# Reordering the opening of a two-layer diffusion-transformer kernel: one weight load, the modulation units, and the key tiles and first query weights in other buffers

## The chip, the cores and the metric

The kernel runs on one core of one Trainium2 chip. The metric is the device time of one execution in microseconds (us). PE is the matrix engine, DVE the vector engine, ACT the scalar engine, POOL the general engine, SP the engine whose queue issues most DMA transfers. SBUF is the on-chip memory in which tiles lie, PSUM the eight accumulator banks that PE writes.

## The reference

Two layers over 512 latent tokens (stream 0 in the kernel) and 256 context tokens (stream 1), width 1024. Layer 0 is windowed attention with grouped keys, layer 1 retention; each is followed by a SwiGLU. The part that the change touches is the beginning of layer 0:

```python
c_act = jax.nn.silu(c)[:, None, :]
cc_act = jax.nn.silu(c_ctx)[None, None, :]
y_ctx = ctx
for i in range(DEPTH):
    mx = jnp.split(c_act @ ada_w[i] + ada_b[i], 6, axis=-1)
    mc = jnp.split(cc_act @ ada_w[i] + ada_b[i], 6, axis=-1)
    h_x = modulate(rms_norm(x, norm1_g[i]), mx[0], mx[1])
    h_c = modulate(rms_norm(y_ctx, norm1_g[i]), mc[0], mc[1])
...
q_x, k_x, v_x = jnp.split(h_x @ w_qkv, [qd, qd + kvd], axis=-1)
q_x = rope_2d(rms_norm(q_x.reshape(B, S, N_HEADS, HEAD_DIM), q_gain), tables)
k_x = rope_2d(rms_norm(k_x.reshape(B, S, N_KV_HEADS, HEAD_DIM), k_gain), tables)
k_c, v_c = jnp.split(h_c @ w_qkv[:, qd:], 2, axis=-1)
k_c = rms_norm(k_c.reshape(B, L, N_KV_HEADS, HEAD_DIM), k_gain)
```

The other four of the six modulation rows (a gate, then shift, scale and gate for the SwiGLU) are needed only behind the attention. Layer 1 also needs the logarithm of its decay, `log_sigmoid(decay_logit)`, for 8 numbers.

## The kernel before, in words

The time to some 100 us is the opening: all inputs of layer 0 come in, the modulation rows are computed on PE, and keys, values and the first queries are projected. Every float32 product of a projection is made of three matmuls, high weight by high input, low weight by high input, high weight by low input (`mm3`, L143 to L149); a weight tile of 128x1024 is split into a high part by ACT (`whi`, L164 or L382) and a low part by DVE (`wlo`, L165 or L386).

The order on PE, DVE and ACT is written out by hand (L469 to L517, in a manual schedule), and after that for PE alone (L642 to L661), where a scheduler orders the other engines. The pieces, with the short names that the text uses:

- A **quarter** (`ada_quarter`, L337) multiplies four loaded 128x1024 tiles by the two conditioning columns, and gives a quarter of the shift and scale rows of both streams. `columns(1)`, which it returns as `c1`, writes those of the context.
- **U0 to U3** (`ada_unit`, L309): 64 small matmuls each (L315), for the other modulation rows; each unit needs 2 MB of weights. ACT copies the result out (L318). **T0 to T3** are what a unit returns (`finish`): one transpose on PE (L322) and two small additions on DVE (L325).
- **K(s,q)** (`keys`, L445) and **V(s,q)** (`values`, L455): a quarter of the depth of the key and value projections of stream s. In the trace they are L450 and L464; the latent keys go to the PSUM tiles `pj`, the context keys to `pO`, the values to `kvv`.
- **KF0, KF1** (`key_factor`, L540): one matmul (shown as 2 pieces, L542) that sums the squares of a key tile, then on ACT a logarithm, an exponential (both L101) and a square (L198), and on DVE three operations (L199, L200, L545). The key gain (L529, L530) copies key tiles out of PSUM, and `rope_key` (L532) rotates the two latent ones in four DVE operations.
- **q0[0], q0[1], ...** are the pieces of the first query projection. q0[0] is 15 matmuls of 128x512 (L147 to L149). Its weight tile comes raw (`q0_raw`) and is split in four half pieces.
- The **lg chain** (L801 to L819): two ACT operations and 21 small DVE operations on 8 columns. The scheduler puts them where their inputs allow.

Loads are all issued by SP, in program order, and an issue that waits for a buffer holds up all behind it. The quarters, two of the four key/value weights and the units U1 to U3 rotate through 8 buffers with the tag `adan` (128x1024 each); the first two key/value weights lie in `wraw` buffers. U0 comes into the 8 buffers with the tag `k`, which hold keys later. PSUM: quarters, units, transposes and key factors take turns in two banks, `pT`.

The loads stand in this order: quarter 0, three key/value weights, quarter 1, the context, the fourth key/value weight, quarters 2 and 3, the rotation tables, the masks, `q0_raw`, then U0 (8 loads) and U1 to U3 (12). `off_grid` (L228) allocates a narrow filler tile, so that the tiles behind it start at another offset.

Of the kernel before, what the change touches and what calls it, by code (L numbers as in the profile page):

```python
# [8 lines left out]
F32 = mybir.dt.float32  # L9
# [40 lines left out]
def dit_kernel(ctx, tc, xT, cT, crow, small, consts, masks, tabs0, tabs1, jtab, adaQ, adaN, adaT, wst, out):  # L50
# [346 lines left out]
    load_w(st_p, "adan", 8)  # L397
# [70 lines left out]

    with tc.manual_schedule(engines={mybir.EngineType.PE, mybir.EngineType.DVE, mybir.EngineType.Activation}):  # L469
        for n in (SX, SX, SX, SX, 256):  # L470
            busy(n)
        stats0(0)
        c1 = ada_quarter(0, wq[0], lambda: busy(256))
        split_w(st_p)
        busy(SX)
        hidden0(0, 0, 1, between=(split_low,))
        c1()
        split_w(st_p)
        split_low()
        keys(0, 0)  # L480
        split_w(rp)
        split_low()
        squares0(1)
        c1 = ada_quarter(1, wq[1], lambda: values(0, 0, (0, 1)))
        hidden0(0, 2, 3)
        c1()
        values(0, 0, (2, 3))
        rms(1, bank=pT)
        keys(0, 1)
        c1 = ada_quarter(2, wq[2], lambda: values(0, 1, (0, 1)))  # L490
        c1()
        hidden0(1, 0, 1)
        split_w(rp)
        hidden0(1, 2, 3)
        values(0, 1, (2, 3))
        c1 = ada_quarter(3, wq[3], lambda: (keys(1, 0), hidden0(0, 4, 5)))
        c1()
        split_low()
        keys(1, 1)
        hidden0(0, 6, 7)  # L500
        keys(0, 2)
        c1 = ada_unit(UNITS[0], wu[0])
        hidden0(1, 4, 5)
        hidden0(1, 6, 7)
        c1()
        values(1, 0)
        values(1, 1)
        c1 = ada_unit(UNITS[1], wu[1])
        for i, mt in enumerate(mtmp):
            nc.vector.tensor_copy(mask[:, 4 * i * P:4 * i * P + mt.shape[1]], mt)  # L510
        keys(1, 2)
        c1()
        c1 = ada_unit(UNITS[2], wu[2])
        keys(0, 3)
        last_key = keys(1, 3)
        c1()
        c1 = ada_unit(UNITS[3], wu[3])  # L517
# [3 lines left out]
    swap16 = [i + 16 if i < 16 else i - 16 for i in range(32)]  # L521


    kx, kc = {}, {}
    kn = [T(ap, 512, "tt", TTB) for _ in range(3)]
    ksq = [T(ap, 656, "pr", PRB)[:, :512] for _ in range(3)]
    off_grid(ap, 16)
    for a, b, o in zip(kn, ksq, (kvx[0], kvc, kvx[1])):
        nc.scalar.activation(b, o, AF.Square)  # L529
        nc.scalar.activation(a, o, AF.Identity, scale=qk_gain[:, 1:2])  # L530

    def rope_key(t):  # L532

        yy = T(ap, 512, "tt", TTB)
        nc.vector.stream_shuffle(yy, t, swap16)
        nc.vector.tensor_tensor(t, t, rope0[:, 0:512], op=mult)
        nc.vector.tensor_tensor(yy, yy, rope0[:, 512:1024], op=mult)
        nc.vector.tensor_tensor(t, t, yy, op=add)
# [8 lines left out]
    def key_parts(e, src, tag="k", bufs=8):  # L547
        k1, k2 = T(akv, 512, tag, bufs, F32R), T(akv, 512, tag, bufs, F32R)
# [10 lines left out]
    def make_q(j, raw=None):  # L559
# [3 lines left out]
        if raw is None:  # L563
            w = next_w(ap, 0)
            parts_of = lambda k: (w[0][:, k * P:(k + 1) * P], w[1][:, k * P:(k + 1) * P])
        else:

            rows = [[T(ap, 656, "pr", PRB, F32R)[:, :512] for _ in range(2)] for _ in range(2)]
            for i, (hi, lo) in enumerate(rows):
                split(raw[:, i * 512:(i + 1) * 512], hi, lo)  # L570
# [70 lines left out]
    q0 = make_q(0, q0_raw)  # L641
    with tc.manual_schedule(engines={mybir.EngineType.PE}):  # L642
        after(values(0, 2), [last_key])
        c1()
        rope_key(kn[0])
        key_factor(0)
        q0[0]()
        key_factor(1)
# [3 lines left out]
        off_grid(akv, 16)  # L652
        for e in range(2):
            k1, k2 = key_parts(e, kn[1], "kc", 4)
            kc[e], kc[2 + e] = ((k1[:, c], k2[:, c]) for c in HALVES)
        off_grid(akv, 48)
# [145 lines left out]
    after(nc.scalar.activation(t1, dec, AF.Abs), [turn["pre"]])  # L802
# [1161 lines left out]
```

## Time and profile before

| what | value |
|---|---|
| median of 3 runs | 1722.77 us (1722.70 to 1722.93) |
| the profiled execution, its own time | 1725.47 us |
| its span, from the first to the last instruction | 1723.7 us |
| mean granted PE clock in it | 0.998 |
| instructions | 27805 |

A row of the timeline gives the start, the duration from the first start to the last end of the row's instructions, the engine, the line, the operation, the tiles written and read, and the count; in brackets stands how long the engine was idle before it, and what ended that. Matmuls are pipelined, so that a row's duration reaches some tenths into the next row: how long a piece of PE work takes is read from start to start.

### The profile page before, as it was taken

The page shows a single profiled execution, that of the slowest core. Times are in us where ns is not written, and L with a number is a line of the kernel's source. Part 1 is how long each engine was busy: PE and PEld are TensorE (multiplying, and loading weights), DVE is VectorE, ACT ScalarE, POOL GpSimd, SP SyncE. Part 2 cuts the span into 40 slices and gives each one's busy share as a digit, 9 for nine tenths or more (in the row PEclk, how much of TensorE's full clock was granted, in tenths as well). Part 3 has the DMA queues.
Part 4 walks back from the last instruction along what each step waited for, and adds up shares of the span by engine and source line. Part 5 has one row for each costly group of instructions (what it writes and reads, how often), then busy time and mean ns, then how long its engine had stood idle before and what let it go on. Part 6 is the DMA issues. An engine that isn't in the chain of part 4 may idle for free.

```text
span 1723.7 us, 27805 instructions
## 1 busy us (share of the span) xinstructions
PE 1697.5 (98%) x10876; PEld 1514.5 (88%) x10876; DVE 1341.2 (78%) x2418; ACT 867.9 (50%) x1550; POOL 65.7 (4%) x186
## 2 busy tenths in 40 slices
PE   7999999999999999999999999999999999999999
PEld 5788877899999999999988888898898999899988
DVE  6698889788778788787879857757767898877774
ACT  5587779565433334242555534534525564445442
POOL 0000000000000000000000000000000000000000
PEclk9999999999999999999999999999999999999999
DMA  9612221633244534343443624625624323333322
GB/s 351 240 30 58 62 62 56 208 125 125 78 152 122 159 110 147 113 149 118 147 127 84 197 87 122 176 67 132 183 70 121 100 74 117 104 110 111 98 86 86
DMA packets 63378, 209.57 MB, mean 122 GB/s; under 512 B 7312, under 2 KB 8976, under 8 KB 62992
## 3 DMA queue, kind: packets, MB, share of 16 engines
q1 hardware_dynamic: 53168, 171.63, 31.1%
q0 software_dynamic: 9792, 35.66, 8.4%
q8 instruction: 85, 1.39, 0.3%
q10 hardware_dynamic: 288, 0.52, 0.1%
q14 instruction: 45, 0.37, 0.1%
HBM read 201.75 MB, written 2.10 MB: 118 GB/s over the span
## 4 chain that ended last, share of the span: by engine, by line
PE 85%; DVE 6%; DMA 6%; ACT 2%; issue 1%; SPq 0%; DVEq 0%; ACTq 0%
PE Y L897 14%; PE Z L897 7%; PE pj L147 7%; PE pj L149 7%; PE pj L148 7%; PE Z L1296 6%; PE Y L1285 3%; PE X L897 3%; DMA wraw<-in_wst_dram 3%; PE pj L1296 3%; PE pT L736 2%; PE pO L750 2%; PE S L710 2%; PE X L1285 2%; PE X L149 1%; PE X L147 1%
## 5 line engine op out<-in xcount | busy, mean ns | idle before, releaser
L164 ACT CAST whi<-wraw 128x1024 fp32r<-128x1024 f32 x264 | 276.3, 1051 | 337.8 <-PE Z L149 81.3
L165 DVE TENSOR_TENSOR wlo<-wraw,whi 128x1024 fp32r<-128x1024 f32 x264 | 321.5, 1221 | 80.2 <-ACT whi L164 78.5
L897 PE MATMUL Y<-aq,whi 128*128 128x384 f32 x640 | 173.6, 335 | 0.2 <-ACT hn L1053 0.2
L897 PEld LDWEIGHTS Y<-aq,whi 128*128 128x128 f32 x640 | 116.6, 188 | 1.7 <-ACT hn L1053 1.4
L256 DVE SCALAR_TENSOR_TENSOR res<-pj,mod,res 128x512 f32<-128x512 f32 (+1 forms) x112 | 81.1, 728 | 39.6 <-PE pj L149 39.2
L897 PE MATMUL Y<-aq,wlo 128*128 128x384 f32 x320 | 107.0, 334 | 0.0
L273 DVE CUSTOM_DVE_ANT_0 y<-adaw,crow,small_sb 128x1024 bf16<-128x1024 f32 x64 | 81.9, 1280 | 31.7 <-DMA adaw<-in_adaT_dram 31.4
L1296 PE MATMUL Z<-whi,sA 128*128 128x512 f32 x256 | 80.9, 391 | 0.0
L101 ACT ACTIVATE pr<-pr,stat,qs 128x513 f32<-128x513 f32 (+2 forms) x96 | 74.2, 774 | 9.1 <-DVE stat L717 8.8
L147 PE MATMUL pj<-ax,whi 128*128 128x512 f32 x176 | 69.2, 393 | 0.9 <-DVE res L256 0.9
L149 PE MATMUL pj<-ax,whi 128*128 128x512 f32 x176 | 68.7, 390 | 0.0
L148 PE MATMUL pj<-ax,wlo 128*128 128x512 f32 x176 | 68.6, 390 | 0.0
L147 PE MATMUL pj<-act,whi 128*128 128x512 f32 x168 | 65.6, 390 | 0.0
L148 PE MATMUL pj<-act,wlo 128*128 128x512 f32 x168 | 65.6, 390 | 0.0
L149 PE MATMUL pj<-act,whi 128*128 128x512 f32 x168 | 65.5, 391 | 0.0
L897 PEld LDWEIGHTS Y<-aq,wlo 128*128 128x128 f32 x320 | 60.1, 188 | 0.0
L711 DVE CUSTOM_DVE_ANT_0 pr<-S,mask,qs 128x256 f32<-128x256 f32 (+1 forms) x96 | 53.1, 566 | 7.9 <-PE S L710 5.4
L897 PE MATMUL Y<-sA,whi 128*128 128x256 f32 x304 | 58.1, 277 | 0.0
L1296 PEld LDWEIGHTS Z<-whi,sA 128*128 128x128 f32 x256 | 48.0, 188 | 10.4
L897 PE MATMUL Y<-hx,whi 128*128 128x256 f32 x304 | 56.3, 277 | 0.0
L736 PE MATMUL pT<-const_sb,pr 128*128 128x128 f32 x352 | 53.7, 278 | 1.2 <-ACT tt L738 0.9
L1296 PE MATMUL Z<-wlo,sA 128*128 128x512 f32 x128 | 50.4, 394 | 0.5 <-DVE wlo L165 0.5
(580 smaller groups left out, 5051.2 us busy)
## 6 DMA issues: line engine op xcount, KB each, us to landing
wraw<-in_wst_dram SPq DMA_DIRECT2D x224, 512.0 KB, 3.7
adaw<-in_adaT_dram POOLq DMA_DIRECT2D x48, 512.0 KB, 3.8
adan<-in_adaQ_dram SPq DMA_DIRECT2D x16, 512.0 KB, 9.0
wx<-in_wst_dram SPq DMA_DIRECT2D x16, 512.0 KB, 6.4
adan<-in_adaN_dram SPq DMA_DIRECT2D x12, 512.0 KB, 7.7
wx<-in_wst_dram POOLq DMA_DIRECT2D x12, 512.0 KB, 7.4
adaw<-in_adaT_dram SPq DMA_DIRECT2D x8, 512.0 KB, 4.0
wraw<-in_wst_dram POOLq DMA_DIRECT2D x8, 512.0 KB, 5.6
```

Source lines behind the costliest of these rows:

```text
L101: ins = nc.scalar.activation(*args, **kw)
L147: nc.tensor.matmul(o, whi, xhi, start=first, stop=False)
L148: nc.tensor.matmul(o, wlo, xhi, start=False, stop=False)
L149: return nc.tensor.matmul(o, whi, xlo, start=False, stop=last)
L164: after(nc.scalar.copy(hi, t), behind)
L165: return nc.vector.tensor_tensor(lo, t, hi, op=sub)
L256: return nc.vector.scalar_tensor_tensor(res[d], o, mods[l, s][:, part, d:d + 1], res[d], mult, add)
L273: res.append(nc.vector.tensor_tensor_reduce(junk, w, cr[:, s * 1024:(s + 1) * 1024], 1.0, sm_t[:, C_ADAB + l * 48 + j:C_ADAB + l * 48 + j ...
L736: nc.tensor.transpose(tp[:, a * P:(a + 1) * P], self.pr[(0, 2, 1, 3)[a]][:, ki * P:(ki + 1) * P], ident)
L897: nc.tensor.matmul(o, p, r, start=first and k + i == 0, stop=k == 3 and i == 2, skip_group_check=not first)
L1285: ins = nc.tensor.matmul(o[:, e * SC:(e + 1) * SC], p[:, ws], r, start=first and k + e + i == 0, stop=k == 3 and i == 2, skip_group_check= ...
L1296: ins = nc.tensor.matmul(os[t], p, r, start=first and k + i == 0, stop=k == 3 and i == 2, skip_group_check=by_k or not first)
```

## The change

- The **fourth key/value weight** is loaded into a buffer with the tag `kc`, which holds context keys later, and no longer into one of the 8 `adan` buffers. To that end `kc` is two tiles of 1024 columns, where it was four of 512, and the two fillers are allocated at this place.
- The **order of the pieces** in the opening is new: U0 stands behind V(1,0) and V(1,1), T0 and U1 behind K(1,2), T1 behind K(0,3), U2 behind K(1,3), T2 behind V(0,2), and U3, with KF0 inside it, behind that. T3 stands between q0[0] and KF1. The context's first columns (`c1`) come behind a split.
- The **key tiles, their squares, the rotation's temporary and the split first query weights** take `res` tiles, which are free since the inputs have been read, and no longer tiles of the attention's pool, which opens only after the staging pool has closed. So the key gain, the rotation of both latent key tiles and the split of the query weights are in the part that is ordered by hand.
- The **lg chain** is made to run behind the mask copies.

On PE, the place behind K(0,2), which ends with the first row of each list (`h`, `hc` are the normed inputs of the two streams, `k` and `adan` unit weights, `ccol` the conditioning columns, `sq` a unit's rows). Before:

```order
L450 MATMUL pj<-h,whi 128x512 x2
L315 MATMUL pT<-k,ccol 32x128 x32
L322 MATMUL pT<-const_sb,sq 128x128
L464 MATMUL kvv<-whi,hc 128x256
L464 MATMUL kvv<-wlo,hc 128x256
```

Of the change, the end of V(1,1) and what follows:

```order
L466 MATMUL kvv<-wlo,hc 128x256
L466 MATMUL kvv<-whi,hc 128x256
L315 MATMUL pT<-k,ccol 32x128 x32
L452 MATMUL pO<-hc,whi 128x256 x2
L452 MATMUL pO<-hc,wlo 128x256 x2
L452 MATMUL pO<-hc,whi 128x256 x4
L452 MATMUL pO<-hc,wlo 128x256 x2
L452 MATMUL pO<-hc,whi 128x256 x2
L322 MATMUL pT<-const_sb,sq 128x128
L315 MATMUL pT<-adan,ccol 32x128 x32
L452 MATMUL pj<-h,whi 128x512 x2
```

U0 has moved behind both value pieces, and K(1,2) stands between it and its transpose, where before nothing did. (This view counts a unit's 64 matmuls as 32.)

On PE again, the place of KF0. Before:

```order
L464 MATMUL kvv<-wlo,h 128x256
L464 MATMUL kvv<-whi,h 128x256
L322 MATMUL pT<-const_sb,sq 128x128
L542 MATMUL pT<-pr,const_sb 128x512
L147 MATMUL pj<-h,pr 128x512
```

Of the change:

```order
L322 MATMUL pT<-const_sb,sq 128x128
L315 MATMUL pT<-adan,ccol 32x128 x24
L553 MATMUL pT<-res,const_sb 128x512
L315 MATMUL pT<-adan,ccol 32x128 x8
L147 MATMUL pj<-h,res 128x512
```

The transpose before KF0 is now T2, and U3, which stood ahead of V(0,2), surrounds KF0. T3 has gone behind the 15 matmuls of q0[0].

On ACT, the stretch from the key gain to the logarithm of KF1 (`whi<-wraw` is the high part of the second query weights). Before:

```order
L530 ACTIVATE tt<-pj,qk_gain 128x512
L164 CAST pr<-wraw 128x512
L164 CAST whi<-wraw 128x1024
L164 CAST pr<-wraw 128x512
L101 ACTIVATE pr<-pT,small_sb 128x512
L101 ACTIVATE pr<-pr 128x512
L198 ACTIVATE pr<-pr 128x512
L101 ACTIVATE pr<-pT,small_sb 128x512
```

Of the change:

```order
L476 ACTIVATE res<-pj,qk_gain 128x512
L318 COPY sq<-pT 128x128
L101 ACTIVATE pr<-pT,small_sb 128x512
L101 ACTIVATE pr<-pr 128x512
L164 CAST whi<-wraw 128x1024
L198 ACTIVATE res<-pr 128x512
L101 ACTIVATE pr<-pT,small_sb 128x512
```

The two halves of the first query weights are gone from here (they are split earlier), U3's copy stands ahead of KF0's logarithm, and the whole cast of the second query weights stands ahead of KF0's square. On DVE the low part of the second query weights (L165, 128x1024) stands right ahead of the first operation of KF0 (L199), as the rows of the change show:

```order
L165 TENSOR_TENSOR wlo<-wraw,whi 128x1024
L199 SCALAR_TENSOR_TENSOR res<-pT,res 128x512
L325 TENSOR_TENSOR mod_74<-pT,small_sb 128x4
L200 SCALAR_TENSOR_TENSOR pr<-res,pr 128x512
L325 TENSOR_TENSOR mod_75<-pT,small_sb 128x4
L556 TENSOR_TENSOR res<-res,pr 128x512
```

L199 reads KF0's sums in PSUM, so KF0's bank is free only behind it.

The diff (`...` marks what is left out):

```diff
--- before.py
+++ after.py
@@ -394,7 +394,9 @@
     load_w(st_p, "adan", 8)
     wq.append(ada_quarter_load(1))
     res0[1] = load_stream(1)
-    load_w(st_p, "adan", 8)
+    off_grid(akv, 16)
+    load_w(akv, "kc", 2)
+    off_grid(akv, 48)
     wq += [ada_quarter_load(2), ada_quarter_load(3)]
     rope0 = T(akv, 1024, "rope0", 1)
     nc.sync.dma_start(rope0.rearrange("p (a n) -> p a n", a=2), tabs0)
@@ -466,6 +468,21 @@
                     first = first or ins
         return first
 
+    swap16 = [i + 16 if i < 16 else i - 16 for i in range(32)]
+    row = lambda dt=F32: T(rp, 512, "res", 12, dt)
+
+    def key_gain(i, o):
+        nc.scalar.activation(ksq[i], o, AF.Square)
+        nc.scalar.activation(kn[i], o, AF.Identity, scale=qk_gain[:, 1:2])
+
+    def rope_key(t):
+
+        yy = row()
+        nc.vector.stream_shuffle(yy, t, swap16)
+        nc.vector.tensor_tensor(t, t, rope0[:, 0:512], op=mult)
+        nc.vector.tensor_tensor(yy, yy, rope0[:, 512:1024], op=mult)
+        nc.vector.tensor_tensor(t, t, yy, op=add)
+
     with tc.manual_schedule(engines={mybir.EngineType.PE, mybir.EngineType.DVE, mybir.EngineType.Activation}):
         for n in (SX, SX, SX, SX, 256):
             busy(n)
@@ -474,9 +491,9 @@
         split_w(st_p)
         busy(SX)
         hidden0(0, 0, 1, between=(split_low,))
-        c1()
         split_w(st_p)
         split_low()
+        c1()
         keys(0, 0)
         split_w(rp)
         split_low()
@@ -499,43 +516,37 @@
         keys(1, 1)
         hidden0(0, 6, 7)
         keys(0, 2)
-        c1 = ada_unit(UNITS[0], wu[0])
+        values(1, 0)
+        values(1, 1)
         hidden0(1, 4, 5)
         hidden0(1, 6, 7)
+        c1 = ada_unit(UNITS[0], wu[0])
+        keys(1, 2)
         c1()
-        values(1, 0)
-        values(1, 1)
         c1 = ada_unit(UNITS[1], wu[1])
         for i, mt in enumerate(mtmp):
-            nc.vector.tensor_copy(mask[:, 4 * i * P:4 * i * P + mt.shape[1]], mt)
-        keys(1, 2)
+            mask_end = nc.vector.tensor_copy(mask[:, 4 * i * P:4 * i * P + mt.shape[1]], mt)
+        q0_rows = [(row(F32R), row(F32R)) for _ in range(2)]
+        for i, (hi, lo) in enumerate(q0_rows):
+            split(q0_raw[:, i * 512:(i + 1) * 512], hi, lo)
+        keys(0, 3)
         c1()
+        last_key = keys(1, 3)
+        kn, ksq = [row(), row(), row()], [row(), row(), row()]
+        key_gain(0, kvx[0])
+        rope_key(kn[0])
         c1 = ada_unit(UNITS[2], wu[2])
-        keys(0, 3)
-        last_key = keys(1, 3)
+        key_gain(1, kvc)
+        key_gain(2, kvx[1])
+        values(0, 2)
         c1()
         c1 = ada_unit(UNITS[3], wu[3])
     St.close()
     At = ExitStack()
     ap = At.enter_context(tc.tile_pool(name="ap", bufs=1, reuse_waits="tile"))
-    swap16 = [i + 16 if i < 16 else i - 16 for i in range(32)]
-
 
     kx, kc = {}, {}
-    kn = [T(ap, 512, "tt", TTB) for _ in range(3)]
-    ksq = [T(ap, 656, "pr", PRB)[:, :512] for _ in range(3)]
     off_grid(ap, 16)
-    for a, b, o in zip(kn, ksq, (kvx[0], kvc, kvx[1])):
-        nc.scalar.activation(b, o, AF.Square)
-        nc.scalar.activation(a, o, AF.Identity, scale=qk_gain[:, 1:2])
-
-    def rope_key(t):
-
-        yy = T(ap, 512, "tt", TTB)
-        nc.vector.stream_shuffle(yy, t, swap16)
-        nc.vector.tensor_tensor(t, t, rope0[:, 0:512], op=mult)
-        nc.vector.tensor_tensor(yy, yy, rope0[:, 512:1024], op=mult)
-        nc.vector.tensor_tensor(t, t, yy, op=add)
 
@@ -545,7 +556,11 @@
         nc.vector.tensor_tensor(kn[i], kn[i], y, op=mult)
 
     def key_parts(e, src, tag="k", bufs=8):
-        k1, k2 = T(akv, 512, tag, bufs, F32R), T(akv, 512, tag, bufs, F32R)
+        if tag == "kc":
+            both = T(akv, 1024, tag, bufs, F32R)
+            k1, k2 = both[:, 0:512], both[:, 512:1024]
+        else:
+            k1, k2 = T(akv, 512, tag, bufs, F32R), T(akv, 512, tag, bufs, F32R)
         src = src[64 * e:64 * e + 64, :]
         nc.scalar.copy(k1[0:64, :], src)
         nc.scalar.copy(k2[64:128, :], src)
@@ -556,18 +571,14 @@
 
     q, stats = {}, {}
 
-    def make_q(j, raw=None):
-
-
-
-        if raw is None:
+    def make_q(j, rows=None):
+
+
+
+        if rows is None:
             w = next_w(ap, 0)
             parts_of = lambda k: (w[0][:, k * P:(k + 1) * P], w[1][:, k * P:(k + 1) * P])
         else:
-
-            rows = [[T(ap, 656, "pr", PRB, F32R)[:, :512] for _ in range(2)] for _ in range(2)]
-            for i, (hi, lo) in enumerate(rows):
-                split(raw[:, i * 512:(i + 1) * 512], hi, lo)
             parts_of = lambda k: [t[:, k % 4 * P:(k % 4 + 1) * P] for t in rows[k // 4]]
         qs = T(ap, 64, "qs", 4)[:, 0:36].rearrange("p (f n) -> p f n", f=3)
         sqs, o = [], [None, None]
@@ -638,22 +649,18 @@
 
         return [first, second, third, norms]
 
-    q0 = make_q(0, q0_raw)
+    q0 = make_q(0, q0_rows)
     with tc.manual_schedule(engines={mybir.EngineType.PE}):
-        after(values(0, 2), [last_key])
-        c1()
-        rope_key(kn[0])
         key_factor(0)
         q0[0]()
+        c1()
         key_factor(1)
         for e in range(2):
             kx[e] = key_parts(e, kn[0])
         q0[1]()
-        off_grid(akv, 16)
         for e in range(2):
-            k1, k2 = key_parts(e, kn[1], "kc", 4)
+            k1, k2 = key_parts(e, kn[1], "kc", 2)
             kc[e], kc[2 + e] = ((k1[:, c], k2[:, c]) for c in HALVES)
-        off_grid(akv, 48)
         q0[2]()
         values(0, 3)
         q0[3]()
@@ -799,7 +806,7 @@
     t1 = cp.tile([P, 8], F32, name="lg_t1")
     t2 = cp.tile([P, 8], F32, name="lg_t2")
     t3 = cp.tile([P, 8], F32, name="lg_t3")
-    after(nc.scalar.activation(t1, dec, AF.Abs), [turn["pre"]])
+    after(nc.scalar.activation(t1, dec, AF.Abs), [turn["pre"], mask_end])
     lnexp(t1, t1, AF.Exp, scale=-1.0)
     nc.vector.tensor_scalar(t2, t1, 2.0, None, op0=add)
     nc.vector.reciprocal(t2, t2)
```

## The prediction, before the result was known

> **What bounds the kernel now.** First the page, for the engines' shares:
>
> ```profile
> span 1723.7 us, 27805 instructions
> PE 1697.5 (98%) x10876; PEld 1514.5 (88%) x10876; DVE 1341.2 (78%) x2418; ACT 867.9 (50%) x1550; POOL 65.7 (4%) x186
> ```
>
> PE is busy for all but 26 us. What an edit of the opening can bring is a part of those 26 us, or of PE time that is stretched. So I read the chain of waits through the opening next (start, duration, what ran):
>
> ```profile
> 15.30 9.36 DMA res<-in_cT_dram
> ...
> 35.24 0.62 PE pT L345 x16
> 35.88 0.33 SPq L334
> ...
> 50.97 9.98 DMA adan<-in_adaN_dram
> ```
>
> It has three parts. First the context's load sets the pace: it lands at 24.68, and its squares and the rest follow. Then PE works up to quarter 2, and at 35.88 SP issues a load that had waited for quarter 2's first matmuls. All later loads stand behind that issue, and the last of them, U2's weights, lands at 60.95. Two stretches (columns: length, busy time and instructions of PE, weight loads, DVE, ACT, POOL, then granted clock, DMA share, GB/s) show the loads' side:
>
> ```profile
> 35.00:38.00 3.00, 3.00 (x74) 2.63 (x73) 0.00 (x0) 0.37 (x1) 0.00 (x0) 1.00 0.46 137
> 45.00:65.00 20.00, 18.25 (x264) 14.55 (x263) 10.46 (x28) 4.82 (x11) 0.00 (x0) 1.00 1.03 413
> ```
>
> Around the late issue the DMA engines are half empty for 3 us (a share of 0.46, so about 1.6 us of transfer lost); from 45 to 65 they are full at 413 GB/s, while PE idles. The third view is PE's timeline, start to start:
>
> ```profile
> 48.59 1.53 PE L315 MATMUL pT<-k,ccol 128*32 128x128 f32 x48
> ...
> 50.94 0.43 PE L315 MATMUL pT<-k,ccol 128*32 128x128 f32 x8 [0.18 <-DMA k<-in_adaN_dram]
> ...
> 51.89 0.36 PE L464 MATMUL kvv<-whi,hc 128*128 128x256 f32 x1
> ...
> 54.89 1.96 PE L315 MATMUL pT<-adan,ccol 128*32 128x128 f32 x64
> 56.77 0.50 PE L450 MATMUL pO<-hc,whi 128*128 128x256 f32 x2
> ...
> 58.49 1.08 PE L315 MATMUL pT<-adan,ccol 128*32 128x128 f32 x32
> ...
> 61.56 0.74 PE L450 MATMUL pj<-h,whi 128*128 128x512 f32 x2
> ...
> 64.46 0.40 PE L450 MATMUL pO<-hc,whi 128*128 128x256 f32 x2
> ...
> 66.08 1.96 PE L315 MATMUL pT<-adan,ccol 128*32 128x128 f32 x64
> 67.96 0.39 PE L464 MATMUL kvv<-whi,h 128*128 128x256 f32 x1
> ...
> 71.05 1.02 PE L542 MATMUL pT<-pr,const_sb 128*128 128x512 f32 x2
> ...
> 72.91 0.51 PE L148 MATMUL pj<-h,pr 128*128 128x512 f32 x1 [0.23 <-DVE pr L165]
> ...
> 76.25 1.02 PE L542 MATMUL pT<-pr,const_sb 128*128 128x512 f32 x2
> ```
>
> An undisturbed unit takes 1.88 us (54.89 to 56.77, and 66.08 to 67.96). U0 with T0 took 3.30 (48.59 to 51.89) and U2 took 3.07 (58.49 to 61.56): these two wait for weights, T0 also for a copy of U0's rows. The third wait is in q0[0], which stands until DVE has made the query weights' low part (72.91).
>
> **The change, part by part.**
>
> *Ahead of 48.59: nothing.* The first columns and the lg chain move out of the way of stream 0, before 24.68. Whatever is won there waits for the same context load, whose place in SP's queue stays. The fourth weight's load and the loads behind it come a little earlier, but PE's work to 48.59 hangs on the context. I take 0; the bounds are 0 and 0.5 us either way.
>
> *From 48.59 to the end of U3: 2.6 us.* The pieces are the same, in the order V(1,0) V(1,1), U0, K(1,2) T0, U1, K(0,3), T1 K(1,3), U2, V(0,2) T2, U3. By the rows above they take 3.00 + 1.88 + 1.72 + 1.88 + 2.90 + 1.62 + 1.88 + 3.09 + 1.88 = 19.85 us if none waits, against 22.46 (48.59 to 71.05). So U3 would end at 68.44 without KF0, instead of 71.05 with T3: 2.61 us. None has to wait for weights: U0's last piece had landed at 50.9 even with the late issue (its matmuls then start, behind the DMA), and U0 is wanted from 51.6 on; U2's at 60.95, and wanted at 61.6 (48.59 + 3.00 + 1.88 + 1.72 + 1.88 + 2.90 + 1.62). The fourth weight's buffer, which lets the loads run some 1.6 us ahead, is only a margin on that. A transpose's copy is covered by the key piece ahead of it.
>
> *KF0 and q0[0]: 0.9 us.* They took 5.20 us (71.05 to 76.25). KF0 is 0.86 and a matmul 0.23 by the chain's rows:
>
> ```profile
> 76.41 0.86 PE pT L542 x2
> 77.27 0.23 PE pj L147
> ```
>
> That makes 0.86 + 15 x 0.23 = 4.31; the rest was the wait for the split, which is now made before 62. So KF1 could start at 68.44 + 4.31 + 0.2 (T3, one matmul of less width, so somewhat less than 0.23) = 72.95, where it stood at 76.25.
>
> *A new wait at KF1: 1.1 us back.* The two `pT` banks are taken in turn by U3, KF0, T3 and KF1, so KF1 gets KF0's bank, and must wait for L199 of KF0 on DVE. What stands ahead of L199 is priced by these rows:
>
> ```profile
> 68.15 0.27 ACT L318 COPY sq<-pT 128x128 f32<-128x128 f32 x1 [6.13 <-PE pT L315]
> 68.31 0.60 ACT L529 ACTIVATE pr<-pj 128x512 f32<-128x512 f32 x1
> ...
> 71.97 1.10 ACT L164 CAST whi<-wraw 128x1024 fp32r<-128x1024 f32 x1
> ...
> 73.44 0.74 ACT L101 ACTIVATE pr<-pT,small_sb 128x512 f32<-128x512 f32 x1
> 74.22 0.63 ACT L101 ACTIVATE pr<-pr 128x512 f32<-128x512 f32 x1
> ```
>
> ```profile
> 73.37 1.22 DVE L165 TENSOR_TENSOR wlo<-wraw,whi 128x1024 fp32r<-128x1024 f32 x1
> ...
> 77.09 0.68 DVE L199 SCALAR_TENSOR_TENSOR pr<-pT,pr 128x512 f32<-128x512 f32 x1
> ```
>
> U3 now ends behind KF0, at 68.44 + 0.86 = 69.30. Its copy starts 0.19 later (68.15 against 67.96), the logarithm 0.16 behind that (69.65), the exponential 0.78 on (70.43), the cast of the second query weights 0.63 on (71.06); it takes 1.10, their low part 1.22, and L199 0.68: 74.1. PE is there at 72.95 and stands for about 1.1 us. KF1 starts at 74.1 and not 76.25: **a lead of 2.15 us**. Behind it q0[1] and the rest stand in the same order on PE as before, and no engine's work there begins at a time of its own; the lead is kept.
>
> *DVE's load, hidden.* DVE now makes the lg chain, the split's low parts and two rotations between 55 and 69. The prices:
>
> ```profile
> 13.97 1.78 DVE L811 SCALAR_TENSOR_TENSOR lg_t<-lg_t,lg_t 128x8 f32<-128x8 f32 x9
> ```
>
> ```profile
> 55.31 0.69 DVE L510 CAST mask<-hn 128x512 bf16<-128x512 f32 x2
> ...
> 69.53 0.75 DVE L535 STREAM_SHUFFLE tt<-tt 128x512 f32<-128x512 f32 x1
> ...
> 71.43 0.69 DVE L536 TENSOR_TENSOR tt<-tt,rope 128x512 f32<-128x512 f32 x1
> ```
>
> T0's additions end near 55.3, the masks at 56.2, the lg chain (21 operations at 0.20) at 60.5, two low parts of 0.69 at 61.9. The first key tile comes from ACT at 62.7; its rotation (0.75 + 3 x 0.69) ends at 65.5, the second one's shuffle at 66.3. T2 reaches DVE at 66.6. So there are about 0.3 us of slack at T2, and 1.1 more until KF0 wants T2's bank (at 68.0, 24 of U3's 32 steps behind 66.56). At the low part (72.2) the slack is 3 us.
>
> *Addresses.* Tiles of the attention's pool start at other offsets, and the trace of before can't show what these cost. The nearest rows are the score products, which read two kinds of key tiles, at different offsets:
>
> ```profile
> L710 PE MATMUL S<-kc,q x192: 274/282/580, 99.8 to 301.6; 128*128 128x256 f32 x192
> L710 PE MATMUL S<-k,q x128: 274/336/449, 99.5 to 301.8; 128*128 128x256 f32 x64, 128*128 128x384 f32 x64
> ```
>
> Their shortest durations agree to the nanosecond. I take 0, and 0.3 us either way.
>
> *The clock.* PE's granted clock falls to a half in one later place, behind a wait for DVE:
>
> ```profile
> 254.49 0.47 PE L710 MATMUL S<-kc,q 128*128 128x256 f32 x2 [2.53 <-DVE qs L620]
> ```
>
> ```profile
> 253.20:256.60 3.40, 1.34 (x6) 0.89 (x6) 3.37 (x16) 1.71 (x4) 0.00 (x0) 1.00 0.13 49
> 256.60:260.00 3.40, 3.21 (x14) 2.85 (x14) 2.89 (x15) 3.34 (x8) 0.00 (x0) 0.50 0.01 2
> ```
>
> The half clock comes behind 3.4 us in which PE was busy for 1.34. With the work 2.15 us earlier the wait of 2.53 lies from about 249.8 to 252.3. If the grid of such stretches stays where it is, it is in the one from 249.8 to 253.2, which is then just as empty: the slow stretch comes too, only sooner in the work. I take 0. If the wait were cut in two by an edge, the slow stretch would go: at most half of 3.4, 1.7 us.
>
> [...]
>
> **The sum.** 2.61 + 0.89 - 0.2 - 1.15 = 2.15 us. Against the profiled execution that is 1725.47 - 2.15 = 1723.3 us, with a span of 1721.5; that execution lies 2.7 us over the median of the runs shown, so against the median it is 1722.77 - 2.15 = **1720.6 us**. A measurement of this kernel can tell about 0.2% from no change, which is 3.4 us: the forecast lies within it.
>
> **The rivals.**
>
> *B, no wait at KF1.* If ACT's casts run sooner, or DVE gets to L199 before the low part, the lead at KF1 is all of 3.3 us: 1719.5. Against it stand the written orders; for it, that the steps of 0.16, 0.78 and 0.63 come from places with other neighbours. 0.13.
>
> *C, the slow stretch goes* with the forecast's lead: 1720.6 - 1.7 = 1718.9. For it, that its place hangs on a tenth of a microsecond at 249.8; against it, that a wait shifted by less than a stretch is empty somewhere. 0.08.
>
> *D, the change doesn't do what it says.* U0 and U2 wait as before, since the loads land later with PE's wait gone from among them, and only q0[0]'s 0.9 is kept (1721.9), or the lead is lost to a later wait (1722.8). For it, DMA at 1.03 of its share; against it, that the loads keep their order, and margins of 0.7 us with the old times. 0.12.
>
> *E, slower: DVE becomes the bound of the opening.* Place: T2's additions, which free KF0's bank. DVE has 12.5 us of work there in the 13.8 us from 55.2 to 69.0. The first 1.4 us of delay (0.3 + 1.1) are free, the next 2.15 eat the lead; from 3.6 us on each costs its own length. If those operations take 40% longer than their rows (5 us), the result is 1.4 us slower: 1724.2; at 60% (7.5 us) it is 1726.7. Against it, the rows of each kind are known. 0.06.
>
> **How the numbers follow.** The forecast has 0.61: 1720.6, with its own unknown terms 1719.8 to 1721.4. The range, 1718.7 to 1723.0, takes in B, C and D, and leaves out E and the far ends of B and C. Faster by over 0.2% means below 1719.3: C and a third of B, 0.12. Slower by over 0.2% means over 1726.2: half of E, 0.03. The rest, 0.85, lies within.
>
> **What would show it.** In the changed profile: the first row of V(1,0) where U0 stood, within 0.5 us of 48.6; no wait longer than 0.2 us for `k` or `adan` in L315; SP issuing the rotation tables well ahead of 36; U3's first row near 66.6, KF0 near 68.0; q0[0]'s rows unbroken; a wait of about 1 us in front of KF1 that DVE's L199 ends, and KF1 at 74.1. The time would be wrong if that lead of 2.15 us isn't found again at the first scores (99.5 before), if PE waits for `pT` at KF0, or if the half clock near 256 has gone.

## The result, and the profile after

| | before | changed |
|---|---|---|
| median of 22 runs | 1723.86 us (1722.01 to 1726.83) | 1721.36 us (1719.92 to 1723.85) |
| ratio, 95% interval | | 0.9985 (0.9979 to 0.9991) |
| profiled execution: own time, span | 1725.47, 1723.7 | 1722.00, 1720.1 |

The change makes the kernel 2.5 us faster by the medians; the interval of the ratio is 1.6 to 3.6 us. The forecast was 2.15 us. (The median of before is 1.1 us above that of its first three runs, so 1721.36 and the predicted 1720.6 differ by more than the two gains do.) The forecast put the change within the 0.2% that it took for the limit of a measurement; it is 0.15% by the medians, and with 22 runs of each the whole interval of the ratio lies below 1. The two profiled spans differ by 3.6 us, and the sections below show how much of that is the change.

The page and the two stretches of the opening, in the changed kernel:

```profile
span 1720.1 us, 27800 instructions
PE 1695.5 (99%) x10876; PEld 1516.3 (88%) x10876; DVE 1342.2 (78%) x2418; ACT 867.4 (50%) x1550; POOL 65.6 (4%) x186
```

```profile
35.00:38.00 3.00, 3.00 (x72) 2.45 (x72) 0.00 (x0) 0.37 (x1) 0.00 (x0) 1.00 1.02 415
45.00:65.00 20.00, 19.84 (x283) 17.37 (x283) 17.71 (x56) 8.42 (x20) 0.11 (x1) 1.00 0.94 367
```

From 35 to 38 the DMA engines are full (a share of 1.02, where it was 0.46), and from 45 to 65 PE is busy for 19.84 us of 20, where it was 18.25. DVE's 17.71 was 10.46: the lg chain, the split and a rotation have come in. SP issues the rotation tables at 29.86, where it was 36.25. PE's timeline:

```profile
48.73 0.28 PE L466 MATMUL kvv<-whi,hc 128*128 128x256 f32 x1
...
51.65 1.95 PE L315 MATMUL pT<-k,ccol 128*32 128x128 f32 x64
53.53 0.50 PE L452 MATMUL pO<-hc,whi 128*128 128x256 f32 x2
...
55.17 0.33 PE L322 MATMUL pT<-const_sb,sq 128*128 128x128 f32 x1
55.42 1.96 PE L315 MATMUL pT<-adan,ccol 128*32 128x128 f32 x64
...
61.74 1.96 PE L315 MATMUL pT<-adan,ccol 128*32 128x128 f32 x64
63.63 0.39 PE L466 MATMUL kvv<-whi,h 128*128 128x256 f32 x1
...
66.80 1.52 PE L315 MATMUL pT<-adan,ccol 128*32 128x128 f32 x48
68.25 1.12 PE L553 MATMUL pT<-res,const_sb 128*128 128x512 f32 x2
69.30 0.65 PE L315 MATMUL pT<-adan,ccol 128*32 128x128 f32 x16
69.88 0.50 PE L147 MATMUL pj<-h,res 128*128 128x512 f32 x1
...
73.44 0.27 PE L322 MATMUL pT<-const_sb,sq 128*128 128x128 f32 x1
74.44 1.12 PE L553 MATMUL pT<-res,const_sb 128*128 128x512 f32 x2 [0.73 <-DVE res L199]
```

Units stand in single rows of 64 without a bracket: U0 takes 1.88 us (51.65 to 53.53) and U2 1.89. q0[0] runs from 69.88 without a wait, and KF0 doesn't wait for its bank. KF1 waits for DVE's L199, as predicted, but for 0.73 us where 1.15 was forecast, and stands at 74.44. ACT and DVE ahead of it:

```profile
70.07 0.27 ACT L318 COPY sq<-pT 128x128 f32<-128x128 f32 x1 [3.90 <-PE pT L315]
70.23 0.69 ACT L101 ACTIVATE pr<-pT,small_sb 128x512 f32<-128x512 f32 x1
70.96 0.63 ACT L101 ACTIVATE pr<-pr 128x512 f32<-128x512 f32 x1
71.50 1.03 ACT L164 CAST whi<-wraw 128x1024 fp32r<-128x1024 f32 x1
```

```profile
72.56 1.23 DVE L165 TENSOR_TENSOR wlo<-wraw,whi 128x1024 fp32r<-128x1024 f32 x1 [3.49 <-ACT whi L164]
73.70 0.68 DVE L199 SCALAR_TENSOR_TENSOR res<-pT,res 128x512 f32<-128x512 f32 x1
```

This is the forecast chain, link by link: its first link comes 0.6 us later than forecast, its last 0.3. How far the lead gets is seen in the score products, whose row gives the first and the last start (99.5 to 301.8 before):

```profile
L717 PE MATMUL S<-k,q x128: 274/337/449, 97.8 to 300.5; 128*128 128x256 f32 x64, 128*128 128x384 f32 x64
```

The lead is 1.7 us at the first and 1.3 at the last. The missing 0.4 and the rest of the 3.6 us come up below.

### The profile page after: what moved, and what is told of

It is laid out like the page before. It is cut to its first block, busy times and chain, and to the rows that moved or that the text cites. A ratio compares the mean times of both kernels' runs of the same rounds, so it can differ in the third digit from the quotient of the medians.

```text
span 1720.1 us, 27800 instructions
## 1 busy us (share of the span) xinstructions
PE 1695.5 (99%) x10876; PEld 1516.3 (88%) x10876; DVE 1342.2 (78%) x2418; ACT 867.4 (50%) x1550; POOL 65.6 (4%) x186
## 4 chain that ended last, share of the span: by engine, by line
PE 90%; DVE 4%; DMA 2%; ACT 2%; issue 1%; SPq 0%; DVEq 0%; ACTq 0%
PE Y L904 16%; PE Z L904 8%; PE pj L147 7%; PE pj L149 7%; PE pj L148 7%; PE Z L1303 7%; PE X L904 4%; PE Y L1292 4%; PE pj L1303 3%; PE pT L743 2%; PE pO L757 2%; PE S L717 2%; PE X L1292 2%; DMA wraw<-in_wst_dram 1%; PE X L149 1%; PE X L147 1%
## 5 line engine op out<-in xcount | busy, mean ns | idle before, releaser
L165 DVE TENSOR_TENSOR wlo<-wraw,whi 128x1024 fp32r<-128x1024 f32 x264 | 321.5, 1222 | 84.1 <-ACT whi L164 82.8
L743 PEld LDWEIGHTS pT<-const_sb,pr 128*128 128x128 f32 x352 | 40.2, 142 | 12.1 <-issue 4.0
```

The source lines that it names most:

```text
L165: return nc.vector.tensor_tensor(lo, t, hi, op=sub)
L743: nc.tensor.transpose(tp[:, a * P:(a + 1) * P], self.pr[(0, 2, 1, 3)[a]][:, ki * P:(ki + 1) * P], ident)
```

## The experiments

When K(0,2) ends differs between the profiles, from 47.4 to 49.6 us (by 0.3 and 0.9 us between two profiles of one kernel). So absolute places in the expectations below, such as "KF1 at 74.4", are met or missed by this shift too, and the opening is compared by the **stretch from the end of K(0,2) to KF1**: 27.66 us before (48.59 to 76.25) and 25.71 in the changed kernel (48.73 to 74.44). Every ratio below is to runs of the kernel before on the same chip, with its 95% interval; 0.0009 of it is 1.6 us, so that these intervals can't tell one version from the next. The stretch is read from one profile of each version; two profiles of one kernel differ in it by 0.24 and 0.04 us.

| kernel | stretch | ratio |
|---|---|---|
| before; once more | 27.66; 27.42 | 1 |
| changed; once more | 25.71; 25.75 | 0.9985 (0.9979 to 0.9991) |
| e1, fourth weight in adan | 25.72 | 0.9992 (0.9984 to 1.0001) |
| e2, kc buffer alone | 25.63 | 0.9986 (0.9977 to 0.9995) |
| e3, T3 behind q0[1] | 24.69 | 0.9981 (0.9972 to 0.9990) |
| e4, query weights split late | 26.38 | 0.9989 (0.9980 to 0.9998) |
| e5, units at their old places | 24.72 | 0.9986 (0.9977 to 0.9995) |
| e6, masks copied five times | 25.69 | 0.9990 (0.9982 to 0.9999) |
| e7, lg chain early | 25.73 | 0.9980 (0.9971 to 0.9989) |
| e8, res tiles and late lg chain alone | 26.13 | 0.9994 (0.9985 to 1.0002) |
| e9, U2 and U3 earlier | 26.18 | 0.9989 (0.9980 to 0.9998) |

### e1: the buffer undone

```diff
-    off_grid(akv, 16)
-    load_w(akv, "kc", 2)
-    off_grid(akv, 48)
+    load_w(st_p, "adan", 8)
```

(The context key tiles are four of 512 columns again.)

> The changed kernel with one part undone: the fourth key/value weight goes back into an adan buffer, and kc is four tiles of 512 again. Theory (the order of the pieces makes the gain, the buffer is only a margin): no wait over 0.3 us for unit weights in L315, U2 near 61.7, KF1 at 74.4 +- 0.3 as in the changed kernel, first score at 97.8 +- 0.3, time equal to the changed kernel's (ratio to before about 0.9985). Rival (the earlier loads make the gain): U2 waits 0.7 us or more, KF1 at 75.2 or later, and more than half of the gain is gone.

The stretch is 25.72 against 25.71 (all of it 1.3 us earlier, since K(0,2) ended at 47.44 here), and PE's view has no wait for a unit's weights:

```profile
60.45 1.95 PE L315 MATMUL pT<-adan,ccol 128*32 128x128 f32 x64
...
73.16 1.13 PE L551 MATMUL pT<-res,const_sb 128*128 128x512 f32 x2 [0.74 <-DVE res L199]
```

With the new order the earlier loads bring nothing: the theory held in the trace. Its clause on the time is not borne out or refuted; the interval reaches from 1.0001 to below the changed kernel's ratio.

### e2: the buffer alone

The kernel before with the diff of e1 the other way round.

> The kernel before with one part of the change: the fourth key/value weight in a kc buffer. Theory: the waits for U0's and U2's weights vanish (0.21 + 0.18 + 0.19 + 0.58 = 1.16 us in the trace of before), T0's wait of 0.44 for its copy and the wait in q0[0] for the low part stay; KF1 at 75.1 +- 0.3, against 76.25 before, first score at 98.4, about 1.1 us faster. Rival (the DMA engines are the limit and the earlier issue moves nothing): KF1 at 76.2, no gain. Rival (the buffer is the whole gain): KF1 at 74.5.

```profile
51.31 0.33 PE L322 MATMUL pT<-const_sb,sq 128*128 128x128 f32 x1 [0.44 <-ACT sq L318]
...
57.97 1.95 PE L315 MATMUL pT<-adan,ccol 128*32 128x128 f32 x64
...
71.21 0.50 PE L148 MATMUL pj<-h,pr 128*128 128x512 f32 x1 [0.23 <-DVE pr L165]
...
74.54 1.02 PE L544 MATMUL pT<-pr,const_sb 128*128 128x512 f32 x2
```

The weights' waits are gone, T0's wait for its copy and q0[0]'s for the low part stay, as the theory had it; but the gain is 2.0 us and not 1.1. I had added the brackets of PE's rows. By starts, U0 with T0 took 2.48 (3.30 before) and U2 1.88 (3.07): 0.82 + 1.19 = 2.01. A bracket is only the time in which nothing was running. Before, the 32 matmuls ahead of U2's first wait took 1.08 us to their last end, where half an undisturbed unit takes 0.94: two breaks cost U0 with T0 0.82 us where their brackets make 0.39, and two cost U2 1.19 where theirs make 0.77. Matmuls in a run overlap (an undisturbed unit's row lasts 1.96 us, and the next piece starts at 1.88); across a bracket they don't.

So the buffer alone does as much for the stretch as the whole change. With e1, where the order does it without the buffer, this shows that the two remove the same weight waits by two routes.

### e8: the res tiles alone

The kernel before with the res tiles and the late lg chain; loads and PE's order as before.

> Only the res tiles and the later lg chain: fourth weight in adan, kc four tiles, PE in the order of before (T3 ahead of KF0). Theory: all weight waits of before stay, KF0 at 71.05 +- 0.3, q0[0] without its wait, so KF1 at 75.4 +- 0.3, without a bank wait since T3 stands between; about 0.9 us faster than before. Rival (DVE's added work or the chain behind KF0 eats it): KF1 at 76.2, no gain.

```profile
59.12 0.64 PE L315 MATMUL pT<-adan,ccol 128*32 128x128 f32 x16 [0.53 <-DMA adan<-in_adaN_dram]
...
70.38 1.02 PE L551 MATMUL pT<-res,const_sb 128*128 128x512 f32 x2
...
74.69 1.02 PE L551 MATMUL pT<-res,const_sb 128*128 128x512 f32 x2
```

KF0 to KF1 takes 4.31 us, to the hundredth what the prediction worked out, where it took 5.20: the term of 0.89 is right. U2 still waits for its weights. KF0 came at 70.38 and not at 71.05: U0's weights came in time in this execution, and it took 2.48 us with T0 where it took 3.30; U2 took 3.42 where it took 3.07. That makes 0.47 of the remaining 0.64 us (27.66 - 26.13 - 0.89), and the value and key pieces, some hundredths shorter each, make the other 0.17. The loads are those of before, and the second profile of before has one wait for U0's weights where the first has two, so that this part varies without an edit.

### e5: the units at their old places

```diff
         keys(0, 2)
+        c1 = ada_unit(UNITS[0], wu[0])
+        hidden0(1, 4, 5)
+        hidden0(1, 6, 7)
+        c1()
         values(1, 0)
         values(1, 1)
-        hidden0(1, 4, 5)
-        hidden0(1, 6, 7)
-        c1 = ada_unit(UNITS[0], wu[0])
-        keys(1, 2)
-        c1()
         c1 = ada_unit(UNITS[1], wu[1])
...
+        keys(1, 2)
+        c1()
+        c1 = ada_unit(UNITS[2], wu[2])
         keys(0, 3)
-        c1()
         last_key = keys(1, 3)
...
-        c1 = ada_unit(UNITS[2], wu[2])
+        c1()
+        c1 = ada_unit(UNITS[3], wu[3])
         key_gain(1, kvc)
         key_gain(2, kvx[1])
         values(0, 2)
-        c1()
-        c1 = ada_unit(UNITS[3], wu[3])
```

> The changed kernel with the units at their places of before (U0 and T0 ahead of V(1,0), U1 ahead of K(1,2), U2 ahead of K(0,3), U3 ahead of V(0,2)); the kc buffer, the res tiles and T3 behind q0[0] are kept. Theory (KF1's wait for its bank is the bound of this stretch, and DVE's and ACT's chain behind KF0 sets KF1): T0 waits 0.6 to 0.8 us for its copy, but KF0 ends within 0.3 us of where it ends in the changed kernel, and KF1 still stands at 74.5 +- 0.3, with a bank wait of about 0.7; time as the changed kernel's. Rival (each wait removed from PE counts in full): KF1 at 75.1 or later.

Neither theory nor rival: the stretch is 24.72, a microsecond **shorter** than in the changed kernel.

```profile
50.51 0.33 PE L322 MATMUL pT<-const_sb,sq 128*128 128x128 f32 x1 [0.44 <-ACT sq L318]
...
68.42 1.02 PE L553 MATMUL pT<-res,const_sb 128*128 128x512 f32 x2
...
72.83 1.02 PE L553 MATMUL pT<-res,const_sb 128*128 128x512 f32 x2
```

```profile
65.64 0.27 ACT L318 COPY sq<-pT 128x128 f32<-128x128 f32 x1 [3.70 <-PE pT L315]
...
67.91 1.08 ACT L164 CAST whi<-wraw 128x1024 fp32r<-128x1024 f32 x1
69.48 0.69 ACT L101 ACTIVATE pr<-pT,small_sb 128x512 f32<-128x512 f32 x1 [0.49 <-PE pT L553]
```

```profile
71.94 0.68 DVE L199 SCALAR_TENSOR_TENSOR res<-pT,res 128x512 f32<-128x512 f32 x1
```

T0 waits for its copy, as expected, and KF0 comes 20.3 us behind K(0,2)'s end, where it is 19.5 in the changed kernel. But with U3 ahead of V(0,2) ACT copies U3's rows almost 3 us before KF0, and makes the cast of the second query weights while PE is still at the values: at 67.91, ahead of KF0's logarithm. The cast no longer stands between that logarithm and the square, L199 ends at 72.62, and KF1 follows at 72.83 without a wait, with 0.2 us to spare. My theory had kept the changed kernel's order on ACT, which the scheduler doesn't. So the wait at KF1 hangs on the place of U3 around KF0, and **the new order of the units costs the stretch 1.0 us once the buffer is there**. The times can't show this: the ratio is 0.9986, the changed kernel's 0.9985.

### e3: T3 behind q0[1]

```diff
         q0[0]()
-        c1()
         key_factor(1)
         for e in range(2):
             kx[e] = key_parts(e, kn[0])
         q0[1]()
+        c1()
```

> The changed kernel with T3 moved from behind q0[0] to behind q0[1], so that KF1 gets U3's bank, not KF0's. Theory (KF1 waits for L199 only because of the bank): no wait at KF1, KF1 at 73.5 +- 0.2 where it stood at 74.44, first score at 97.0 +- 0.3 (97.81), 0.7 to 0.8 us faster than the changed kernel. Rival (the wait only moves on, to T3 or to the first scores): first score at 97.7, no gain.

```profile
73.02 1.02 PE L553 MATMUL pT<-res,const_sb 128*128 128x512 f32 x2
...
77.02 0.27 PE L322 MATMUL pT<-const_sb,sq 128*128 128x128 f32 x1
```

KF1 waits no more. The stretch is 24.69, 1.02 us shorter, of which 0.27 is T3's own time (73.44 to 74.44 in the changed kernel, less the wait of 0.73), which comes later; at the first score product 0.67 us is left (48.41 from K(0,2)'s end, 49.08 in the changed kernel). U3's place is the same as in the changed kernel, and L199 still ends behind KF1's start (73.29 + 0.68 = 73.97 against 73.02). Only KF1's bank differs: it was the bank.

### e4: the query weights split late

```diff
-        q0_rows = [(row(F32R), row(F32R)) for _ in range(2)]
-        for i, (hi, lo) in enumerate(q0_rows):
-            split(q0_raw[:, i * 512:(i + 1) * 512], hi, lo)
+        [(row(F32R), row(F32R)) for _ in range(2)]
...
+    q0_rows = [[T(ap, 656, "pr", PRB, F32R)[:, :512] for _ in range(2)] for _ in range(2)]
+    for i, (hi, lo) in enumerate(q0_rows):
+        split(q0_raw[:, i * 512:(i + 1) * 512], hi, lo)
```

> The changed kernel with the first query weights split late again, in tiles of the attention's pool; everything else as changed. Theory: ACT makes the two half casts and the whole cast ahead of KF0's logarithm, so q0[0] waits 1.0 to 1.5 us for the low part, and KF0's L199 ends 0.6 to 0.9 us later; KF1 at 75.2 +- 0.3, about 0.8 us slower than the changed kernel. Rival (the early split is worth its whole 0.9 plus the bank wait): KF1 at 75.8 or later. Rival (hidden): KF1 at 74.4.

```profile
71.63 0.50 PE L147 MATMUL pj<-h,pr 128*128 128x512 f32 x1 [0.96 <-ACT pr L164]
72.35 0.50 PE L148 MATMUL pj<-h,pr 128*128 128x512 f32 x1 [0.23 <-DVE pr L165]
...
75.83 1.03 PE L551 MATMUL pT<-res,const_sb 128*128 128x512 f32 x2
```

(The four `res` tiles stay allocated, unused.) The stretch is 26.38, 0.67 us longer: q0[0] waits 0.96 + 0.23, and the bank's wait at KF1 has gone, since PE is late itself. The two waits don't add.

### e6 and e7: DVE's load

```diff
-        for i, mt in enumerate(mtmp):
+        for i, mt in 5 * list(enumerate(mtmp)):
```

> The changed kernel with the two mask copies made five times on DVE, which puts about 2.5 us more of work ahead of the lg chain, the low parts and the rotations (the result is the same). By the working of the prediction DVE has 1.4 us of room there, so KF0 would be 1.1 us late, and KF1 at 75.5. By the trace of the changed kernel the room is larger (2.0 us idle before the second rotation, and 1.1 until KF0 wants the bank): KF0 at 68.2 and KF1 at 74.4, no loss.

The stretch is 25.69. From the first mask copy to the lg chain it is 3.02 us on DVE, where it was 0.60: 2.4 us more of DVE work cost nothing. The prediction's room of 1.4 us was too small, and the trace of the changed kernel shows why:

```profile
59.49 0.68 ACT L476 ACTIVATE res<-pj,qk_gain 128x512 f32<-128x512 f32 x1
```

```profile
66.21 0.01 DVE L481 LOAD_MASK_SELECT res<-res  x1 [2.03 <-ACT res L476]
```

The first key tile's gain is done on ACT at 60.2 (I had 62.7): ACT starts on the tile at 59.00, while PE still works on K(0,3)'s second tile. DVE is through with the first rotation at 64.2 and then waits 2.03 us for the second tile. e7 takes the lg chain out of its new place:

```diff
-    after(nc.scalar.activation(t1, dec, AF.Abs), [turn["pre"], mask_end])
+    after(nc.scalar.activation(t1, dec, AF.Abs), [turn["pre"]])
```

> The changed kernel with the lg chain free to run early again, as before. Theory (hidden at both places): K(0,2) ends at 48.6 +- 0.3 and KF1 stands at 74.4 +- 0.3; no difference in time. Rival (the chain delays stream 0, or its move frees the opening): the rows ahead of 48.7 come 0.4 us later or more.

K(0,2) ends at 48.83 and the stretch is 25.73. That part of the change does nothing here.

### e9: U2 and U3 earlier

```diff
         c1()
+        c1 = ada_unit(UNITS[2], wu[2])
         last_key = keys(1, 3)
...
         rope_key(kn[0])
-        c1 = ada_unit(UNITS[2], wu[2])
+        c1()
+        c1 = ada_unit(UNITS[3], wu[3])
         key_gain(1, kvc)
         key_gain(2, kvx[1])
         values(0, 2)
-        c1()
-        c1 = ada_unit(UNITS[3], wu[3])
```

(T3 stands as in e3. In PE's order KF0 and the first matmul of q0[0] come along: they stand inside U3, and so ahead of V(0,2): KF0 at 66.33, V(0,2) from 68.16.)

> The changed kernel with U2 ahead of K(1,3), T2 and U3 ahead of V(0,2), and T3 behind q0[1]; the kc buffer and the res tiles as changed. Counted from the end of K(0,2) to KF1 (27.66 in the kernel before, 25.71 in the changed one, 24.72 with the old places of the units), theory (with U3 ahead of V(0,2), ACT's chain behind KF0 runs while PE works on the values, and no bank is waited for): 23.4 to 23.9 us, no wait over 0.2 us on PE in between, first score about 1.7 us earlier than in the changed kernel, ratio to before about 0.997 to 0.998. Rival (U2's weights aren't there yet, or KF0 waits for T2's bank): a wait in L315 or at KF0, and 24.5 or more.

The rival came:

```profile
66.33 1.10 PE L553 MATMUL pT<-res,const_sb 128*128 128x512 f32 x2 [1.42 <-DVE mod L325]
```

```profile
63.24 0.75 DVE L481 STREAM_SHUFFLE res<-res 128x512 f32<-128x512 f32 x1
...
65.97 0.23 DVE L325 TENSOR_TENSOR mod<-pT,small_sb 128x4 f32<-128x4 f32 x2
```

KF0 waits 1.42 us for T2's bank, which T2's additions free; they stand on DVE behind the first rotation. That rotation starts at 63.24, where it was 61.40 in the changed kernel, since ACT's order now puts U2's copy (61.85) ahead of the first key tile's square and gain (from 62.01). This is the place that the prediction named for its slower case. There a small operation holds up PE as soon as T2 comes before the rotation's end; in the changed kernel T2 comes late enough. Without that wait the stretch would be some 24.76 (26.18 - 1.42, an estimate), no better than e3 or e5. A version with T2's additions ahead of the rotation wasn't tried.

### e10 and e11: both kernels once more

> The kernel before once more, unchanged, for its profile alone. Theory (the stretches of half clock near 256 us and the differences behind 280 us vary from execution to execution): K(0,2) end to KF1 within 0.3 us of 27.66, but the number of slow stretches near 256 may be one, two or three by where the 3.41 us grid falls, and the time from 280 us to the end differs from the first profile's by up to 2 us. Rival (they belong to the kernel): one slow stretch, and the same time from 280 us on within 0.3 us.

> The changed kernel once more, unchanged, for its profile alone. Theory: K(0,2) end to KF1 within 0.2 us of 25.71, with the bank wait of 0.7 us at KF1; the slow stretches near 256 us and the time behind 280 us as chance has it. Rival: two slow stretches, and the same time from 280 us on within 0.3 us.

The stretches repeat within 0.24 and 0.04 us. What lies behind doesn't. The score products of e10 (before), e1 and e11 (changed):

```profile
L710 PE MATMUL S<-k,q x128: 274/337/445, 99.5 to 302.3; 128*128 128x256 f32 x64, 128*128 128x384 f32 x64
```

```profile
L713 PE MATMUL S<-k,q x128: 274/337/580, 96.4 to 300.4; 128*128 128x256 f32 x64, 128*128 128x384 f32 x64
```

```profile
L717 PE MATMUL S<-k,q x128: 274/337/449, 98.7 to 301.2; 128*128 128x256 f32 x64, 128*128 128x384 f32 x64
```

The first score product comes 1.7 us earlier in the first profiles (99.5 and 97.8) and 0.8 in the second (99.5 and 98.7), since K(0,2) ended at 48.73 and 49.62 in the two of the changed kernel. From K(0,2)'s end it is 50.9 and 50.7 us before, and 49.1 in both of the changed kernel: a lead of 1.6 to 1.8 us.

From the first product to the last it is 202.3 us in the first profile of before and 202.8 in the second, 202.7 and 202.5 in those of the changed kernel, and 204.0 in e1. And from the last product to the end of the span it is 1421.9 (1723.7 - 301.8) and 1422.4 (1724.7 - 302.3) before, 1419.6 and 1421.9 in the changed kernel. The instructions there are the same in both, and one kernel's two profiles differ by 2.3 us. So of the 3.6 us between the two spans, the opening holds 1.7 by the first score product, and the rest can't be put down to the change.

## Why the prediction was right, point by point

1. **Nothing ahead of 48.59**: held on the whole. K(0,2) ends at 48.59 and 48.85 before, at 48.73 and 49.62 after; e7 shows the lg chain to be without weight. The 49.62 lies outside the 0.5 us that the prediction allowed; it goes with a half clock at 30 us, which the first profile of the changed kernel doesn't have there (last section).
2. **2.6 us from 48.59 to the end of U3**: the waits have gone, as said. U3's last 16 rows stand at 69.30, and would end 1.05 us (68.25 to 69.30) earlier without KF0: 69.88 - 1.05 - 48.73 = 20.10 us, where 19.85 was forecast and 22.46 was before. The size was right within 0.25 us. Of this, 0.17 is K(1,2) with T0 (53.53 to 55.42, 1.89 for 1.72): T0 waits 0.2 us for its copy, which ACT makes only at 54.87, behind its work on the context's inputs. So "a transpose's copy is covered by the key piece ahead of it" was not quite true. Another 0.15 is U3, cut in two by KF0. But "only a margin" is half of the truth on the buffer: e2 shows that it would have removed these waits without the new order, and e1 that the order does without it.
3. **0.9 us in q0[0]**: right; e8 gives 0.89.
4. **1.1 us back at KF1**: the mechanism was right, and e3 shows that the bank is the cause. The wait is 0.73 us by its bracket and 0.75 by e3 (1.02 less 0.27 for T3), where 1.15 was forecast. Term by term the stretch was to be 19.85 + 0.86 (KF0) + 3.45 (q0[0]) + 0.2 (T3) + 1.15 = 25.51 us, and is 20.10 + 1.05 + 3.56 + 0.27 + 0.73 = 25.71: a lead of 1.95 us and not 2.15. PE's terms came out 0.62 too small together, and the wait 0.42 too large. This is only in part luck: KF1 starts when L199 ends, so that what q0[0] and T3 take more comes off the wait. What U3's end loses (0.25 + 0.19) does count, and the luck is that the chain from there to L199's end took 4.50 us where 4.8 had been added up from other places. The prediction took U3's place as given and didn't ask what ACT could have done ahead of it; e5 answers that.
5. **DVE hidden**: right, with a room that was sized 1.0 us or more too small (e6: 2.4 us for 1.4).
6. **Addresses: nothing**: not contradicted. The shortest score product takes 274 ns before and after, the median one 336 and 337.
7. **The clock costs nothing**: right as an expectation of the difference between the kernels, wrong as a picture. In the changed kernel's profile the slow stretch lasts twice as long (6.83 us for 3.41), and goes with 0.3 to 0.4 us less of a lead; in e10 the kernel before has it twice as long as well. Rival C had it that a shift can only remove it; no run shows it gone, nor the 1.7 us: all 13 profiles have it, and in the changed kernel's the clock falls inside the wait for DVE, at 252.2.
8. **The lead is kept to the end**: it is there at the first scores, 1.6 to 1.8 us from K(0,2)'s end, where 2.15 was forecast. The medians differ by 2.5 us with an interval of 1.6 to 3.6, which holds the opening's 1.7 to 1.95 as well as the forecast; so the time by itself confirms the size only roughly. Whether anything beyond the opening is gained is open.

## What to carry to other kernels

Two edits that remove the same wait don't add up: measure each alone, and together, since here the buffer with the res tiles (e5) does in the opening what the whole change does and 1 us more. When tiles or banks are taken in turn, moving one small user (T3 here) changes who waits for whom: write down the turn, and ask for each bank who frees it and what stands ahead of that on its engine. Judge edits of a microsecond by a stretch of the trace between two fixed instructions, and not by the whole time, which varied by 4 to 6 us among runs of one kernel here.

## What the runs showed of the hardware

PE's granted clock falls to a half between 250.8 and 256.6 us in all 13 profiles, for 3.41, 6.83 or 10.24 us. In the first profiles of the two kernels this is during or soon behind a wait for DVE: before, the wait of 2.53 us ends at 254.49 and the clock falls at 256.6; in the changed kernel the wait of 2.54 us ends at 252.79 and the clock falls at 252.2. Stretches of the changed kernel (PE busy, weight loads, DVE, ACT, POOL, then the granted clock):

```profile
249.80:253.20 3.40, 0.86 (x6) 0.69 (x4) 2.93 (x9) 1.42 (x4) 0.00 (x0) 0.85 0.50 154
253.20:256.60 3.40, 3.23 (x13) 2.61 (x13) 3.40 (x19) 3.08 (x8) 0.00 (x0) 0.50 0.01 2
256.60:260.00 3.40, 2.65 (x14) 2.15 (x12) 1.75 (x8) 3.14 (x9) 0.00 (x0) 0.65 0.03 7
```

And of e1, where it lasts longest:

```profile
253.20:256.60 3.40, 3.40 (x14) 3.04 (x14) 3.19 (x17) 3.08 (x9) 0.00 (x0) 0.50 0.01 2
256.60:260.00 3.40, 2.75 (x12) 2.38 (x13) 1.15 (x4) 2.76 (x8) 0.00 (x0) 0.50 0.02 5
260.00:263.40 3.40, 3.35 (x21) 2.38 (x21) 3.12 (x13) 3.13 (x9) 0.71 (x4) 0.70 0.00 0
```

One slow stretch goes with 202.3 to 202.5 us from the first score product to the last, two with 202.6 to 202.8, three with 203.9 to 204.1: the second goes with some 0.35 us, the third with 1.3 more. Counting when the clock fell in each execution's own work (its time plus its lead at the first score product over the first profile of before), the 13 profiles sort without exception: falls that come at 253.9 to 254.6 last two stretches, at 254.9 to 255.2 three, at 255.5 to 256.8 one. The instructions are the same there, so the likely reason is the place of a 3.41 us grid against the work, which differs from execution to execution of one kernel; no run set it on purpose. The grid is read from the lengths, which are one, two and three times 3.41 us, and from the two half clocks of each kernel's first profile: they begin at 21.07 and 256.59 before, 235.52 us apart, and at 20.07 and 252.17 in the changed kernel, 232.10 us apart, which is 69 and 68 times 3.413.

A half clock of 3.41 us also comes in the opening, in 9 of the 13 profiles: at 19.7 to 22.6 us in seven, and at 29.8 and 29.9 in e11 and e4. In these two the clock granted from 30 to 33 us was 0.50, where it is 1.00 in the first profile of the changed kernel, and K(0,2) ends latest, at 49.62 and 49.45; in the other eleven it ends between 47.44 and 48.91. That the half clock makes it late is likely, but no run shows it apart from this.
